# Stick-breaking values on the seven-product scheme, one weave over the mixer, and the mLSTM output kept in memory for a while

## The chip, the core and the metric

The kernel runs on one core of a Trainium2 chip, in one launch. The metric is the device time of the launch in microseconds; of the kernel before, three timed runs are shown and their median stands for it. The engines are named as in the profile: PE (matmuls, with PEld for its weight loads), DVE, ACT, POOL and SP; a "q" behind a name is the engine's queue, and almost all DMAs are issued from SP's. SBUF is the memory on the chip next to the engines, PSUM the buffers into which PE writes.

## The reference

One layer of a trunk over 256 positions of width 2048, all in float32: a SwiGLU block (2048 to 5632 and back), a layer norm, a mixer, a layer norm, a second SwiGLU block, a layer norm, and a gated embedding. The change lies in the mixer:

```
proj = x @ w_in                                   # (256, 2048) x (2048, 11272)
mq, mk, mv, mo, mi, mf, sq, sk, sv, ga, gb = split_cols(proj)
q_m, k_m = split(silu(causal_conv([mq, mk])))
h    = mlstm(q_m, k_m, mv, gates of mi, mf)       # 4 heads of 256
y_m  = head_norm(h) * sigmoid(mo)                 # (256, 1024)
y_sb = stick_breaking(sq, sk, sv)                 # 8 heads of 128, (256, 1024)
merged = sigmoid(ga) * (y_m @ w_up_m) + sigmoid(gb) * (y_sb @ w_up_sb)
mix = merged @ w_out
```

The stick-breaking attention needs, for each head, all of its q and k before its logits, and its v (sv) in its last product. The mLSTM needs its q, k, v and gates, and mo at its end.

## The kernel before, in words

**A unit of PE work.** Each float32 operand is split into a high and a low half, and a product takes three matmuls (high by high, high by low, low by high; lines 1209 to 1211). The smallest piece of the program is a `Unit`: one weight tile of 256 rows by up to 512 columns against 128 positions, which is 2 x 3 matmuls. A weight tile arrives by one DMA of 512 KB into a raw tile (`loads`, line 1132), ACT writes its high half (line 1160) and DVE its low half (line 1164). Both 128-position tiles use it, so in a plain `group` one load and one split serve two units.

**The seven-product scheme** (`seven`, `both7`) does two column groups of 512 over all 2048 rows with seven products of 2 x 2 blocks in place of eight: 7 x 4 = 28 units in place of 32. Each unit there has a weight tile of its own, and most of these tiles are sums that DVE makes in place (line 349). It also needs sums of the activations (`forms`), which `forms_later` makes from the tiles of x1T (lines 295 to 312). While such a block runs, five PSUM buffers hold its accumulators, and its results are put together from PSUM by ACT (line 400) and DVE (lines 384 and 390).

**The order.** `program` is one list of units and small callbacks. The code runs through it once and emits the instructions of every engine in that order. `sched` holds generators (the steps of an mLSTM head, a stick-breaking head, a transpose); each yields an estimated delay, and its next step is emitted when the units emitted so far add up to that time (line constants in `DELAY`). `until` runs steps early when a unit needs their result. `weave(main, side)` spreads the units of a side list evenly among those of a main list, by their numbers.

**The mixer before.** In a row, as plain groups: q and k of the mLSTM with the gates and the first stick-breaking heads, then v (two groups, line 795), mo (two groups), the first four heads of sv (line 683), and stick-breaking heads; the forms of x1T are made while these run; then the other half of sv. Only then comes the weave: main is the last stick-breaking columns, the gates of merge group 0, and the up products of groups 0 to 2 (`ups`), and side is the gates of groups 1 to 3 as three seven-product blocks (`pair`). The up products of group 3, the transposes of the merged groups (`merge_turn`) and w_out follow. The mLSTM heads run in two chains over the plain groups, and stick-breaking in two chains of four heads, at least 14 planned us apart, from before the weave until inside it.

**Buffers.** 48 SBUF pages of 4 KB per partition (`PAGES`) hold raw and split weights, activations and all the large tiles; a tile keeps its page until its last use. `HELD` limits the raw tiles and split pairs at a time: 5 and 6 in the mode "mix", 7 and 6 in "wide", which is that of the weave. Six `temp` tiles serve the small steps. PSUM has eight buffers (`PSUM_BUFS`), for accumulators and small steps (`misc`) alike. Early in the mixer the residual goes to DRAM and returns before w_out (`put_away`, line 252, and `bring_back`, line 260, on SP's queue).

**Lines of the small steps.** Stick-breaking: logits 888, running sums 901 and 902, their subtraction 903 on DVE, the output product 912, its halves 916 on ACT and 918 on DVE. mLSTM: the output product 844, its denominators 845 to 848 on DVE, the scaling out of PSUM on ACT (a call of line 228), transposes 870, halves 228 and 876. Transposes of q and k of stick-breaking: 693, with the copies 698.

Of the kernel before, what the change touches and what calls it, by code (L numbers as in the profile page):

```python
# [13 lines left out]
P = 128  # L14
# [29 lines left out]

STICK_GAP = 14.0
# [3 lines left out]
    "alpha": 24.0, "away": 5.0, "sig": 1.5, "form": 18.0, "ln_turn": 3.6, "ln_step": 2.1, "gb": 14.0, "h": 8.0, "silu": 6.0, "late": 9.0, "rest": 1.2, "mt": 3.2,  # L49
# [127 lines left out]
def kernel(  # L177
# [156 lines left out]
    def seven(wa, ca, wb, cb, rows, cols, act, done, loaded):  # L334
# [44 lines left out]
    def both7(w, ca, cb, act, dest, ready, loaded):  # L379
# [296 lines left out]
    def sb_columns(ps, t, heads):  # L676

        n = len(heads) * DS
        if heads[0] >= 16:
            if ("sv", t) not in st:  # L680
                st["sv", t] = big()
            c0 = (heads[0] - 16) * DS
            nc.scalar.copy(st["sv", t][:, c0:c0 + n], ps[:, :n])
            flags.update(("sv", t, h - 16) for h in heads)
        else:
            stage = temp()
            nc.scalar.copy(stage[:, :n], ps[:, :n])
            sched.spawn(sb_turn(t, stage, heads), DELAY["sbt"])
# [128 lines left out]

    def mlstm(h):
# [19 lines left out]
        r = small.tile([P, TT], F32, name="hr", tag="hr")  # L838
        hs = temp().rearrange("q (t e) -> q t e", t=TT)
        for t in range(TT):  # L840
            ps = misc([P, DM + 1])
            for s in range(t + 1):
                off = s * 256 + (t - s) * P
                nc.tensor.matmul(ps[:], d[:, off:off + P], st["v", s, h // 2][:, h % 2], start=(s == 0), stop=(s == t))  # L844
            nc.vector.tensor_scalar(out=r[:, t:t + 1], in0=ps[:, DM:], scalar1=-1.0, scalar2=st["em"][:, t, h:h + 1],
                                    op0=ALU.mult, op1=ALU.max)
            nc.vector.tensor_tensor(out=r[:, t:t + 1], in0=ps[:, DM:], in1=r[:, t:t + 1], op=ALU.max)
            nc.vector.reciprocal(out=r[:, t:t + 1], in_=r[:, t:t + 1])
            yield DELAY["m2"]
            activate(hs[:, t], ps[:, 0:DM], ACT.Copy, scale=r[:, t:t + 1])  # L850
# [79 lines left out]
    for which, g in ((0, 1), (1, 0), (1, 1)):  # L930
        program.extend(flat(group(w_in, range(0, D, 2 * P), which * 1024 + g * COL, COL, x1T, qk_done(which, g))))
    program.append(lambda: [sched.spawn(in_sequence([mlstm(a), mlstm(a + 1)])) for a in (0, 2)])
    for g in range(2):
        program.extend(flat(group(w_in, range(0, D, 2 * P), 2048 + g * COL, COL, x1T, v_done(g))))
    for g in range(2):
        program.extend(flat(group(w_in, range(0, D, 2 * P), 3072 + g * COL, COL, x1T, mo_done(g))))
    def sb(*heads):
        if heads[0] >= 16:
            col0 = sq0 + heads[0] * DS
        else:  # L940
            col0 = [(sq0 + h * DS, 2 * DS) for h in heads[::2]]
# [24 lines left out]
    def up_done(g, half):  # L966
        def done(ps, t):
# [3 lines left out]
            if half:  # L971
                m = gt[g, t][:, 0:COL]
                nc.vector.tensor_tensor(out=m, in0=m, in1=a, op=ALU.add)
# [4 lines left out]
    def merge_turn(g, t):  # L978
        transposed(gt[g, t], mergedT, g, t)
        return  # L980
        yield
# [4 lines left out]
    def ups(g):  # L986
        return (flat(group(w_up_m, range(0, HM * DM, 2 * P), g * COL, COL, ymT, up_done(g, 0)))
                + flat(group(w_up_sb, range(0, HS * DS, 2 * P), g * COL, COL, ysbT, up_done(g, 1))))
# [17 lines left out]
    def pair(g):  # L1006
        return both7(w_in, ga0 + g * COL, ga0 + D + g * COL, x1T, gate_dest(g), gate_ready(g), False)
# [239 lines left out]
```

## Time and profile before

| what | value |
| --- | --- |
| three runs | 2199.74, 2199.25, 2196.62 us; median 2199.25 us |
| the profiled execution's own time | 2198.95 us |
| its span, first to last instruction | 2196.9 us, so 2.05 us lie around it |
| mean granted PE clock | 0.999 |
| busy PE, DVE, ACT | 99%, 85%, 59% of the span |
| mLSTM q, k, gates (accumulators read) | 724 to 807 us |
| v, mo, sv, first stick-breaking columns | 808 to 1003 us |
| the weave | 1003 to 1283 us |
| last up products, w_out | 1283 to 1397 us |

The stages are read from the times at which ACT and DVE read the accumulators of each group. A line of the window view gives a stretch, its length, and for PE, PEld, DVE and ACT the busy time and, in brackets, the instructions, then the granted clock, the DMA engines' share and GB/s. A line of the group view gives the line, engine, operation, tiles, shapes and count, then busy us in total, mean ns of one, the idle time of the engine before them and who ended it.

### The profile page before, as it was taken

What the parts mean: (1) busy time and instruction counts of PE and PEld (TensorE: products, weight loads), DVE (VectorE), ACT (ScalarE), POOL (GpSimd) and SP (SyncE); (2) the same over time, 40 slices, a digit from 0 to 9 for tenths busy, and PEclk for the clock granted to TensorE, in tenths of its full rate; (3) what the DMA queues carried; (4) which work ended last, traced back from release to release, by engine and by line L of the source; (5) the groups of instructions that cost most, each with busy time, mean ns of one, the idle gap of its engine ahead of it and who ended that gap; (6) DMA issues with size and microseconds to landing.
All of it is one profiled execution on the core that took longest, in us unless ns stands there. A gap on an engine that the chain in (4) does not pass through costs nothing.

```text
span 2196.9 us, 28181 instructions
## 1 busy us (share of the span) xinstructions
PE 2183.5 (99%) x9990; PEld 1806.0 (82%) x9990; DVE 1867.9 (85%) x2073; ACT 1296.9 (59%) x1576; POOL 100.1 (5%) x88
## 2 busy tenths in 40 slices
PE   9999999999999999999999999999999999999999
PEld 7888888888888888888878888888888888878888
DVE  6999999999987864568978985699999899989774
ACT  7556566565655755565766554565665565656372
POOL 0100010000010000000000000000010000000000
PEclk9999999999999999999999999999999999999999
DMA  9899999999993765665768886589999999899553
GB/s 336 253 304 302 280 286 316 307 307 264 320 334 103 244 215 159 173 182 168 240 190 264 265 282 211 179 244 303 297 282 293 315 293 306 275 299 344 195 168 100
DMA packets 298893, 560.12 MB, mean 255 GB/s; under 512 B 18008, under 2 KB 39424, under 8 KB 298752
## 3 DMA queue, kind: packets, MB, share of 16 engines
q1 hardware_dynamic: 276992, 516.38, 70.8%
q0 software_dynamic: 21760, 41.95, 11.1%
q8 instruction: 78, 1.28, 0.2%
q14 instruction: 63, 0.52, 0.1%
HBM read 554.06 MB, written 4.19 MB: 254 GB/s over the span
## 4 chain that ended last, share of the span: by engine, by line
PE 66%; DVE 3%; DMA 3%; issue 1%; ACT 0%; POOL 0%; DVEq 0%; POOLq 0%; SPq 0%; ACTq 0%
PE mm L1209 21%; PE mm L1210 21%; PE mm L1211 21%; DMA raw<-in_ffn_w_dram 3%; DVE split L1164 2%; DVE raw L349 1%; PE ms L278 1%; PE ms L483 0%; ACT split L1160 0%; PE ms L888 0%; PE ms L832 0%; PE ms L844 0%; PE ms L912 0%; PE ms L901 0%; PE ms L693 0%
## 5 line engine op out<-in xcount | busy, mean ns | idle before, releaser
L1160 ACT CAST split<-raw 128x1024 fp32r<-128x1024 f32 (+2 forms) x1049 | 1046.2, 1037 | 512.6 <-DVE raw L349 171.0
L1164 DVE TENSOR_TENSOR split<-raw,split 128x1024 fp32r<-128x1024 f32 (+2 forms) x1049 | 1224.2, 1202 | 143.0 <-ACT split L1160 129.9
L1209 PE MATMUL mm<-split,actT 128*128 128x512 f32 (+2 forms) x3128 | 1219.9, 390 | 3.2 <-DVE temp L903 2.5
L1210 PE MATMUL mm<-split,actT 128*128 128x512 f32 (+2 forms) x3128 | 1206.2, 386 | 2.4 <-DVE split L1164 2.2
L1211 PE MATMUL mm<-split,actT 128*128 128x512 f32 (+2 forms) x3128 | 1206.5, 386 | 0.6 <-DVE actT L285 0.6
L1210 PEld LDWEIGHTS mm<-split,actT 128*128 128x128 f32 x3128 | 588.7, 188 | 120.4 <-DVE split L1164 7.5
L1211 PEld LDWEIGHTS mm<-split,actT 128*128 128x128 f32 x3128 | 588.0, 188 | 121.0 <-DVE actT L285 1.4
L1209 PEld LDWEIGHTS mm<-split,actT 128*128 128x128 f32 x3128 | 588.3, 188 | 119.2 <-issue 3.6
L349 DVE TENSOR_TENSOR raw<-raw 128x1024 f32<-128x1024 f32 x224 | 273.3, 1220 | 2.4 <-DMA raw<-in_w_in_dram 0.2
L1137 POOL DMA_DIRECT2D raw<-in_ffn_w_dram x80 | 95.5, 1193 | 1867.1 <-DVE temp L547 800.7
L280 ACT CAST actT<-ms 128x512 fp32r<-128x512 f32 x60 | 35.0, 585 | 87.0 <-PE ms L278 86.7
L556 DVE TENSOR_TENSOR temp<-mm,temp 128x512 f32<-128x512 f32 x112 | 76.9, 687 | 5.3 <-PE mm L1211 3.5
L609 DVE SCALAR_TENSOR_TENSOR big<-mm,big 128x512 f32<-128x512 f32 x96 | 65.5, 685 | 16.2 <-PE mm L1211 16.1
L285 DVE TENSOR_TENSOR actT<-ms,actT 128x512 fp32r<-128x512 f32 x60 | 40.8, 685 | 21.2 <-ACT actT L280 11.7
L224 ACT ACT_TABLE_LOAD x33 | 42.3, 1283 | 0.6
L273 DVE TENSOR_TENSOR actT<-temp,actT 128x512 fp32r<-128x512 f32 x40 | 26.5, 688 | 17.3 <-ACT actT L272 17.2
L228 ACT ACTIVATE temp<-mm 128x512 f32<-128x512 f32 (+1 forms) x22 | 12.3, 560 | 44.6 <-PE mm L1211 44.6
L272 ACT CAST actT<-temp 128x512 fp32r<-128x512 f32 x40 | 24.1, 621 | 13.8 <-DVE temp L296 11.9
L228 ACT ACTIVATE temp<-temp 128x512 f32<-128x512 f32 (+1 forms) x48 | 28.5, 593 | 2.2 <-DVE temp L556 1.7
L228 ACT ACTIVATE rstd<-mv,eps 128x1 f32<-128x1 f32 x6 | 1.8, 295 | 46.1 <-DVE mv L466 46.1
L782 DVE SCALAR_TENSOR_TENSOR temp<-ms,cw,temp 128x253 f32<-128x253 f32 (+2 forms) x48 | 22.4, 480 | 7.5 <-ACT temp L228 6.3
L1026 DVE SCALAR_TENSOR_TENSOR big<-big,mm 128x512 f32<-128x512 f32 x8 | 5.5, 687 | 26.9 <-PE mm L1211 26.9
(128 smaller groups left out, 557.4 us busy)
## 6 DMA issues: line engine op xcount, KB each, us to landing
raw<-in_ffn_w_dram SPq DMA_DIRECT2D x655, 512.0 KB, 6.3
raw<-in_w_in_dram SPq DMA_DIRECT2D x168, 512.0 KB, 4.4
raw<-in_ffn_w_dram POOLq DMA_DIRECT2D x80, 512.0 KB, 8.8
raw<-in_w_out_dram SPq DMA_DIRECT2D x32, 512.0 KB, 4.9
raw<-in_w_in_dram SPq DMA_DIRECT2D x56, 256.0 KB, 3.1
raw<-in_w_ple_gate_dram SPq DMA_DIRECT2D x24, 512.0 KB, 4.9
raw<-in_w_up_m_dram SPq DMA_DIRECT2D x16, 512.0 KB, 5.5
raw<-in_w_up_sb_dram SPq DMA_DIRECT2D x16, 512.0 KB, 5.6
```

Source lines behind the costliest of these rows:

```text
L224: nc.scalar.preload_act_table_set(table[0])
L228: nc.scalar.activation(out, in_, func, **kw)
L285: nc.vector.tensor_tensor(out=dst[:, 1], in0=ps[:], in1=dst[:, 0], op=ALU.subtract)
L349: nc.vector.tensor_tensor(out=out.tile[:, :, :cols], in0=a.tile[:, :, :cols], in1=b.tile[:, :, :cols], op=ALU.add)
L556: nc.vector.tensor_tensor(out=out, in0=a, in1=b, op=op)
L609: nc.vector.scalar_tensor_tensor(out=xs, in0=ps, scalar=0.5, in1=xs, op0=ALU.mult, op1=ALU.add)
L1137: nc.gpsimd.dma_start(out=r.tile[:, :, :r.cols], in_=r.plus[0], accum_op=ALU.add)
L1160: nc.scalar.copy(hi[:, ks], r[:, ks])
L1164: nc.vector.tensor_tensor(out=lo[:, ks], in0=r[:, ks], in1=hi[:, ks], op=ALU.subtract)
L1209: nc.tensor.matmul(ps, hi, w[0][:, k, :u.cols], start=first, stop=False)
L1210: nc.tensor.matmul(ps, hi, w[1][:, k, :u.cols], start=False, stop=False)
L1211: nc.tensor.matmul(ps, lo, w[0][:, k, :u.cols], start=False, stop=last)
```

## The change

- sv is no longer computed in two plain groups of 16 units each, whose results ACT copied. It becomes one seven-product block of 28 units (`both7(w_in, sv0, sv0 + COL, ...)`), with destination and readiness callbacks of its own.
- The weave starts earlier: behind the q and k groups. Main is v, mo, the stick-breaking columns, the gates of group 0 and the up products of groups 0 to 2; side is the block of sv and the three gate blocks. Mode "wide" holds from there.
- The forms of x1T are made one group earlier, 14 planned us apart instead of 18.
- The stick-breaking chains start behind the second group of mo.
- In the mLSTM the output product is copied out of PSUM by ACT with its denominators, and the reciprocal and the scaling follow from SBUF.
- When both halves of a tile of the mLSTM's output are ready, it goes to DRAM (four DMAs on SP's queue), and comes back ahead of the first up products, whose stick-breaking half now runs first in group 0.
- The merged groups share tiles: group 1 is written beside group 0 and group 3 beside group 2.
- The delay before a gate's sigmoid is 5.0 in place of 1.5.

```diff
-        if heads[0] >= 16:
...
-            nc.scalar.copy(st["sv", t][:, c0:c0 + n], ps[:, :n])
...
+    def put_ym_away(c, t):
+        nc.sync.dma_start(out=ym_rows(c, t), in_=ymT.tiles.pop((c, t))[:].bitcast(F32))
...
+    def bring_ym_back():
+        for c in range(2):
+            for t in range(TT):
+                ymT.tiles[c, t] = act_tile()
+                nc.sync.dma_start(out=ymT.tiles[c, t][:].bitcast(F32), in_=ym_rows(c, t))
...
-            nc.vector.tensor_scalar(out=r[:, t:t + 1], in0=ps[:, DM:], scalar1=-1.0, scalar2=st["em"][:, t, h:h + 1],
-                                    op0=ALU.mult, op1=ALU.max)
-            nc.vector.tensor_tensor(out=r[:, t:t + 1], in0=ps[:, DM:], in1=r[:, t:t + 1], op=ALU.max)
-            nc.vector.reciprocal(out=r[:, t:t + 1], in_=r[:, t:t + 1])
+            nc.scalar.copy(hs[:, t], ps[:, 0:DM])
+            nc.scalar.copy(den[:, t:t + 1], ps[:, DM:])
             yield DELAY["m2"]
-            activate(hs[:, t], ps[:, 0:DM], ACT.Copy, scale=r[:, t:t + 1])
+        nc.vector.tensor_scalar(out=r[:], in0=den[:], scalar1=-1.0, scalar2=None, op0=ALU.mult)
+        nc.vector.tensor_tensor(out=r[:], in0=den[:], in1=r[:], op=ALU.max)
+        nc.vector.tensor_tensor(out=r[:], in0=r[:], in1=st["em"][:, :, h], op=ALU.max)
+        nc.vector.reciprocal(out=r[:], in_=r[:])
+        yield DELAY["m2"]
+        for t in range(TT):
+            activate(hs[:, t], hs[:, t], ACT.Copy, scale=r[:, t:t + 1])
...
+            if ymT.ready(h // 2, t):
+                sched.spawn(put_ym_away(h // 2, t), DELAY["away"])
...
+    program.append(lambda: [sched.spawn(forms_later(x1T, c), FORMS + 14.0 * c) for c in range(4)])
...
-    program.extend(sb(16, 17, 18, 19))
-    program.append(lambda: [sched.spawn(forms_later(x1T, c), 6.0 + 18.0 * c) for c in range(4)])
-    program.extend(sb(8, 9, 2, 3))
...
+    def merged(g, t):
+        return gt[g // 2 * 2, t][:, g % 2 * COL:(g % 2 + 1) * COL]
...
-    program.append(sticks)
-    program.extend(sb(10, 11, 4, 5) + sb(20, 21, 22, 23))
-    main = sb(12, 13, 6, 7) + sb(14, 15) + branch(0, 0) + branch(0, 1) + ups(0) + ups(1) + ups(2)
+    main = columns(2048, v_done(0)) + columns(3072, mo_done(0)) + columns(2048 + COL, v_done(1)) + sb(8, 9, 2, 3)
+    main += columns(3072 + COL, mo_done(1)) + [sticks] + sb(10, 11, 4, 5) + sb(12, 13, 6, 7) + sb(14, 15)
+    main += branch(0, 0) + branch(0, 1) + [bring_ym_back] + ups(0, True) + ups(1) + ups(2)
+    sv0 = sq0 + 2 * HS * DS
+    side = both7(w_in, sv0, sv0 + COL, x1T, sv_dest, sv_ready)
     mode("wide")
-    program.extend(weave(main, pair(1) + pair(2) + pair(3)))
+    program.extend(weave(main, side + pair(1) + pair(2) + pair(3)))
```

More of the change, by code (lines that the diff above doesn't have):

```diff
@@ L332, in group, with seven @@
         return pairs
-    def seven(wa, ca, wb, cb, rows, cols, act, done, loaded):
+    def seven(wa, ca, wb, cb, rows, cols, act, done, loaded=False):
         n = rows // (4 * P)
@@ L678, in sb_columns @@
         n = len(heads) * DS
-        if heads[0] >= 16:
-            if ("sv", t) not in st:
-                st["sv", t] = big()
-            c0 = (heads[0] - 16) * DS
-            nc.scalar.copy(st["sv", t][:, c0:c0 + n], ps[:, :n])
[L684 to L688, printed above, removed]
+        stage = temp()
+        nc.scalar.copy(stage[:, :n], ps[:, :n])
+        sched.spawn(sb_turn(t, stage, heads), DELAY["sbt"])
     def sb_turn(t, stage, heads):
@@ L838, in mlstm @@
         r = small.tile([P, TT], F32, name="hr", tag="hr")
+        den = small.tile([P, TT], F32, name="den", tag="den", bufs=2)
         hs = temp().rearrange("q (t e) -> q t e", t=TT)
@@ L929, with columns, sv_dest, sv_ready @@
     program.extend(flat(group(w_in, range(0, D, 2 * P), 4096, 2 * HM + 2 * DS, x1T, gates_done)))
[L930 to L931 removed]
+    def columns(col0, done):
+        return flat(group(w_in, range(0, D, 2 * P), col0, COL, x1T, done))
+    program.extend(columns(COL, qk_done(0, 1)) + columns(1024, qk_done(1, 0)))
+    program.append(lambda: [sched.spawn(forms_later(x1T, c), FORMS + 14.0 * c) for c in range(4)])
+    program.extend(columns(1024 + COL, qk_done(1, 1)))
     program.append(lambda: [sched.spawn(in_sequence([mlstm(a), mlstm(a + 1)])) for a in (0, 2)])
[L933 to L936, printed above, removed]
     def sb(*heads):
[L938 to L941, printed above, removed]
+        col0 = [(sq0 + h * DS, 2 * DS) for h in heads[::2]]
         return flat(group(w_in, range(0, D, 2 * P), col0, len(heads) * DS, x1T,
                           lambda ps, t: sb_columns(ps, t, heads)))
[L945 to L947 removed]
+    def sv_dest(k, t):
+        if ("sv", t) not in st:
+            st["sv", t] = big()
+        return st["sv", t][:, k * COL:(k + 1) * COL]
+    def sv_ready(k, t):
+        flags.update(("sv", t, h) for h in range(4 * k, 4 * k + 4))
     def sticks():
@@ L970, in done @@
             nc.vector.tensor_tensor(out=a, in0=ps, in1=a, op=ALU.mult)
-            if half:
-                m = gt[g, t][:, 0:COL]
-                nc.vector.tensor_tensor(out=m, in0=m, in1=a, op=ALU.add)
+            if last:
+                nc.vector.tensor_tensor(out=merged(g, t), in0=gt[g, t][:, 0:COL], in1=gt[g, t][:, COL:], op=ALU.add)
                 if g == 3:
@@ L978, in merge_turn @@
     def merge_turn(g, t):
-        transposed(gt[g, t], mergedT, g, t)
+        transposed(merged(g, t), mergedT, g, t)
         return
```

25 lines of the change are left out of this document (18 added, 7 removed).

## The prediction

> **What bounds the kernel now.** I read the page first, then the view of busy time by stretches, then the chain of waits and the time line around the places where PE stood.
>
> ```profile
> PE 2183.5 (99%) x9990; PEld 1806.0 (82%) x9990; DVE 1867.9 (85%) x2073; ACT 1296.9 (59%) x1576; POOL 100.1 (5%) x88
> ```
> ```profile
> 100.00:600.00 500.00, 499.61 (x2234) 411.96 (x2232) 473.70 (x466) 300.04 (x319) 41.68 (x35) 1.00 0.97 297
> 808.00:1003.00 195.00, 195.00 (x885) 160.15 (x884) 119.24 (x197) 108.58 (x155) 0.00 (x0) 1.00 0.59 167
> 1003.00:1283.00 280.00, 276.76 (x1279) 229.90 (x1277) 251.19 (x271) 180.05 (x226) 0.00 (x0) 0.99 0.76 232
> 808.00:1283.00 475.00, 471.76 (x2163) 390.05 (x2161) 370.43 (x468) 288.63 (x381) 0.00 (x0) 1.00 0.69 206
> ```
>
> PE is the bound: it stands for only 13.4 us (2196.9 - 2183.5), so time falls only with PE's own work or with those 13.4 us. In the plain groups (808 to 1003 us) PE never stands and DVE is busy 61% (119.24 / 195). In the weave (1003 to 1283) DVE is busy 90% and PE loses 3.24 us. The price of one matmul of 512 columns is read from starts in the time line:
>
> ```profile
> 1087.17 0.39 PE L1209 MATMUL mm<-split,actT 128*128 128x512 f32 x1
> ...
> 1090.12 0.39 PE L1210 MATMUL mm<-split,actT 128*128 128x512 f32 x1
> ```
>
> Thirteen steps lie between them: 2.95 / 13 = 0.227 us each (the 0.39 overlaps the next one and is no price), so a unit of six costs 1.36 us. The places where PE stood, by stretches, the last row inside the third:
>
> ```profile
> 1050.00:1060.00 10.00, 9.26 (x56) 7.99 (x56) 7.56 (x9) 7.64 (x15) 0.00 (x0) 1.00 0.64 186
> 1060.00:1080.00 20.00, 20.00 (x120) 17.61 (x119) 19.67 (x22) 13.07 (x20) 0.00 (x0) 1.00 0.83 251
> 1130.00:1140.00 10.00, 7.58 (x35) 6.04 (x33) 9.89 (x10) 4.62 (x5) 0.00 (x0) 1.00 0.80 253
> 1140.00:1150.00 10.00, 9.93 (x37) 8.03 (x38) 6.64 (x8) 4.36 (x7) 0.00 (x0) 0.83 0.37 102
> 1142.00:1144.00 2.00, 2.00 (x6) 1.60 (x5) 2.00 (x4) 1.04 (x1) 0.00 (x0) 0.50 0.54 88
> ```
>
> From 1130 to 1140 DVE is busy 9.89 of 10 us and PE loses 2.42. The chain of waits says why:
>
> ```profile
> 1135.85 1.23 DVE split L1164
> ...
> 1138.24 1.22 DVE split L1164
> 1139.46 0.47 DVE temp L903
> 1139.94 0.14 issue
> 1140.07 0.47 PE mm L1209
> ```
>
> A stick-breaking subtraction (903), which frees a PSUM buffer, stands in DVE's queue behind weight splits, and PE's next accumulator needs a buffer. Of the eight, the seven-product block holds five and the main group two, so one is left for all small steps. The time lost: 0.74 (1050 to 1060) + 2.42 + 0.07, and in the third row 17% of 10 us at the lower clock, 1.7: together **4.9 us**. The clock's row shows 0.50 behind a gap of 2.5 us. (The Trainium skill, "TensorE: Matmul & The Clock Gate", section "What's actually happening", has PE fall to half its clock after an idle window of about 3.4 us. By that rule this gap would have cost no clock and the 4.9 would be 3.2; the measured 0.50 decides.)
>
> **The change, part by part.**
>
> ```profile
> L1164 DVE TENSOR_TENSOR split<-raw,split 128x1024 fp32r<-128x1024 f32 x195 | 233.7, 1220 | 66.3 <-ACT split L1160 62.3 <-PE mm L1210 3.2
> L349 DVE TENSOR_TENSOR raw<-raw 128x1024 f32<-128x1024 f32 x48 | 58.5, 1219 | 0.5 <-DMA raw<-in_w_in_dram 0.2
> L384 DVE TENSOR_TENSOR big<-mm,big 128x512 f32<-128x512 f32 x18 | 12.4, 686 | 0.2
> L1160 ACT CAST split<-raw 128x1024 fp32r<-128x1024 f32 x197 | 200.7, 1050 | 72.8 <-DVE raw L349 26.4 <-PE mm L1210 16.0 <-DVE split L1164 14.2
> ```
>
> *sv by seven products.* 32 units become 28: 4 x 6 x 0.227 = **5.4 us less of PE**, the only certain term, since PE is the bound. Against it: 28 weight tiles are split in place of 16, 12 x 1.22 = 14.6 us of DVE and 12 x 1.05 = 12.6 of ACT; 16 sums of weights, 16 x 1.22 = 19.5 of DVE; and results put together in 7 DVE instructions of 0.686, 4.8. So DVE gets 39 us, ACT 13 (less three copies). Loads rise from 16 to 24.
>
> *One weave.* Main grows from 112 to 208 units, side from 84 to 112. What hides the 39 us of DVE is PE's time over the longer weave: with the mLSTM's small saving (below), (370.4 + 37.5) / (475 - 10) = 88%, against the weave's 90% before and 95% in the first SwiGLU (473.7 / 500), where PE stood for 0.39 us in 500. More to the point is the worst place. A side unit costs DVE 1.22 + 16/28 x 1.22 + 7/28 x 0.686 = 2.09 us. In the half-wide group (heads 14, 15) 16 main units of half price come with 12 side units before: DVE 8 x 0.69 + 12 x 2.09 = 30.6 us to PE's 16 x 0.68 + 12 x 1.36 = 27.2, or 112%, which is the full DVE from 1060 on. After, 8.6 side units come with them: 23.5 to 22.6, 104%. In an up group (16 main units, six DVE results) it was 39.0 to 38.1, 102%, and becomes 31.9 to 33.5, 95%. So DVE's queue should be short where stick-breaking's small steps wait in it, and I take the 4.9 us as gone. What is late next is again a PSUM buffer in the half-wide group.
>
> *mLSTM in the weave.* PE's work is the same. Three small DVE operations for each tile become four for each head:
>
> ```profile
> L845 DVE TENSOR_SCALAR hr<-ms,em 128x1 f32<-128x1 f32 x8 | 1.7, 219 | 16.6 <-PE ms L844 16.6
> L848 DVE RECIPROCAL hr<-hr 128x1 f32<-128x1 f32 x8 | 1.3, 165 | 0.3
> L687 ACT COPY temp<-mm 128x256 f32<-128x256 f32 x2 | 0.7, 362 | 0.0
> ```
>
> 24 operations of about 0.18 become 16: 1.4 us less. ACT gets eight copies of 256 columns (0.36) and eight of one (not shown; at most that 0.36): 3 to 6 us, at 288.6 + 16 of 465 busy, 66%, hidden behind PE. These copies free the PSUM buffer without DVE. The head takes two planned steps longer; nothing waits for it before the up products. But its PSUM steps now stand where seven buffers are taken: the risk of this part.
>
> *Output in memory.* Eight DMAs of 512 KB on SP's queue, with eight more loads of sv: 16 x 0.52 = 8.4 MB to 206 GB/s x 475 us = 98 MB, so 229 GB/s where the first SwiGLU runs at 297. Raw loads queue behind them. The residual is the nearest, waits of SP from 700 to 820 and 1150 to 1310 us:
>
> ```profile
> SPq L252 <- DVE big L511: 13.9, 3, 5.7
> SPq L260 <- PE mm L1211: 0.4, 1, 0.4
> raw<-in_w_in_dram SPq DMA_DIRECT2D x168, 512.0 KB, 4.4
> ```
>
> 5.7 us at the longest, where seven raws at 2.2 us each (200 loads in some 440 us) last 15: nothing on the path. Without that cover PE would lose the wait itself, up to 5.7 each.
>
> *Order.* The forms' 17 us of DVE move ahead of 840 us, where the plain groups left DVE 39% idle; they are planned at 10 to 52 us behind q and k, and needed from about 50 on. Stick-breaking has 72 + 43 = 115 units x 1.297 planned us = 149 until the up products read it, and its chains need 108 + 31 = 140. Both cost nothing; if the chains were late, `until` would emit steps early and PE would stand for them. Packing the merged groups and the sigmoid's delay change places and times, not work.
>
> *New waits.* The trace does not show mLSTM inside a weave, so it is bounded from both sides. Below: the first SwiGLU's 0.4 us. Above: the old rate for each buffer taken.
>
> ```profile
> L888 PEld LDWEIGHTS ms<-big 128*128 128x128 f32 x24 | 4.1, 190 | 1.3 <-ACT big L698 1.0
> L901 PE MATMUL ms<-temp,tri 128*128 128x384 f32 x12 | 4.8, 485 | 0.0
> ```
>
> The old weave had six logits, six sums, eight outputs and four transposes, 24 takes, for 4.9 us. The new one has 24 of stick-breaking, 8 transposes and 4 x 6 of mLSTM, 56: 11.4 us. By DVE's share (88%) the nearest row is the old weave, but its worst places fall by 7 or 8 points; I take half of what it lost, **2.5 us**.
>
> **Sum** against the profiled execution: 2198.95 - 5.4 - 4.9 + 2.5 = 2191.1; the median of the runs stands 0.3 above that execution, so 2191.4, said as **2191 us**. If the waits merely stay as they are, 2198.95 - 5.4 = 2193.5, still faster.
>
> **The rivals.** *Waits at the old rate.* The 56 takes each cost what the 24 did: 2198.95 - 5.4 - 4.9 + 11.4 = 2200. For it: mLSTM's scores (line 834) and its output halves (876) free their buffers only through DVE, so 28 takes wait for DVE in place of 14. Against it: the 95% busy DVE of the first SwiGLU, also with five buffers held and with small steps, cost 0.39 us.
>
> *Raw weights come late: slower.* Where v, mo and the first heads are worked on, the pages asked for are 16 for x1T and its forms, 7 raw, 12 split, 10 of q, k, v and mo, 2 of gates and 2 of sq and sk, 49, and with sv and the first output 53, less those of heads that are done; there are 48. A load that finds no page waits on SP until PE is done with an old split, and fewer loads are under way. From issue to use a raw takes 4.4 + 1.05 + 1.22 + 1.22 = 7.9 us, so at one load in 2.2 us 3.6 must be under way; from three on it decides: 7.9 / 3 = 2.63, 0.43 more for each of the 46 loads between main units 32 and 80, 20 us: 2211. For it:
>
> ```profile
> SPq L1132 <- PE mm L1211: 92.7, 39, 7.5
> DVE raw L349 <- DMA raw<-in_w_in_dram: 0.2, 1, 0.2
> ```
>
> SP does wait for PE's pages (1150 to 1310 us). Against it: by the same count the old weave asks for 52 at 1125 us (16 + 19 + 4 mLSTM outputs + 2 sv + 2 sq, sk + 4 stick-breaking outputs + 5 gates), and in the mixer's weave the engines waited for a load only these 0.2 us; four pages go to memory for the late part.
>
> **How the numbers follow.** The forecast, from 2187 to 2194.8, has 0.68: 5.4 us are sure, and 4.4 us (0.2%, about what a measurement of this kernel can tell from no change) are reached unless waits grow by a us. Waits at the old rate have 0.16, all within 0.2%; late raws 0.16, slower. The low end is the sum with the lowest waits, 2189, less 2 for the spread of runs (2196.62 to 2199.74 before). The high end reaches over the old rate to 2204; most of the late raws and a few hundredths below are left out, under 0.2.
>
> **What would show it.** Right: 24 fewer matmuls of 512 columns, 12 more splits and 16 more sums at line 349; in the half-wide and up groups DVE under full; no granted clock under 1 in the weave; one short wait of PE for a small step's PSUM buffer at most. Old rate: several waits of PE for 903, 918, 834 or 876 with the clock at 0.50 behind them. Late raws: DVE's and ACT's waits for the DMA of raw between 840 and 1000 us, with PE idle in each row there. The prediction is wrong altogether if DVE shows over 95% through the first half of the weave, or PE waits for v or mLSTM steps emitted early.

## The result, and the profile after

The changed kernel takes **2217.15 us** (median of four runs, 2214.71 to 2218.26) beside 2198.51 us for the kernel before (four runs, 2196.62 to 2199.74): ratio 1.0084 [1.0071, 1.0097], 18.6 us slower where 8 us faster was forecast. The profiled execution took 2217.22 us, with a span of 2215.5 us.

The engine totals of the changed kernel, from the first part of its page:

```profile
PE 2185.7 (99%) x9966; PEld 1805.1 (81%) x9966; DVE 1902.6 (86%) x2100; ACT 1313.7 (59%) x1603; POOL 100.1 (5%) x88
```

PE has 24 instructions fewer (9966 for 9990), so the seven-product saving is there; but the span less PE's busy time is now 2215.5 - 2185.7 = 29.8 us, where it was 13.4. Two groups carry DVE's part, the first from the page, the second from the view that keeps shapes apart:

```profile
L1195 DVE TENSOR_TENSOR split<-raw,split 128x1024 fp32r<-128x1024 f32 (+2 forms) x1061 | 1239.9, 1203 | 152.2 <-ACT split L1191 130.2
```
```profile
L352 DVE TENSOR_TENSOR raw<-raw 128x1024 f32<-128x1024 f32 x240 | 293.0, 1221 | 2.8 <-DMA raw<-in_w_in_dram 0.7 <-DMA raw<-in_ffn_w_dram 0.2
```

There are 12 splits more (1061 for 1049) and 16 sums more (240 for 224), as counted, and DVE grew by 1902.6 - 1867.9 = 35 us (39 had been worked out). Now the stretches of the changed kernel's weave, with the columns as told ahead of the prediction:

```profile
840.00:940.00 100.00, 92.54 (x392) 74.52 (x392) 77.94 (x105) 57.70 (x77) 0.00 (x0) 0.95 0.59 179
940.00:1040.00 100.00, 95.68 (x421) 78.26 (x421) 76.76 (x91) 62.49 (x88) 0.00 (x0) 0.97 0.71 220
1040.00:1140.00 100.00, 94.88 (x478) 78.93 (x477) 80.68 (x106) 70.31 (x107) 0.00 (x0) 1.00 0.68 208
1140.00:1240.00 100.00, 96.80 (x432) 79.77 (x432) 77.38 (x87) 61.84 (x76) 0.00 (x0) 1.00 0.75 235
...
1000.00:1020.00 20.00, 15.68 (x60) 11.95 (x59) 12.65 (x18) 11.49 (x19) 0.00 (x0) 0.83 0.43 139
...
1200.00:1283.00 83.00, 83.00 (x369) 68.80 (x368) 76.38 (x75) 47.61 (x51) 0.00 (x0) 1.00 0.84 272
```

The kernel before, in the rows that are not full there:

```profile
1040.00:1140.00 100.00, 96.84 (x485) 81.04 (x483) 86.47 (x99) 69.56 (x98) 0.00 (x0) 1.00 0.74 222
1140.00:1240.00 100.00, 99.93 (x435) 82.59 (x436) 89.30 (x89) 60.01 (x66) 0.00 (x0) 0.98 0.78 243
```

The loss is spread over 840 to 1200 us and is gone from there on, when the mLSTM and stick-breaking heads are done. From 840 to 1240 PE stands for 20.1 us and loses another (0.05 + 0.03) x 100 = 8 us to the lower clock. Before, the same stretch lost 3.2 us and, with rows of 1.00 and 0.98, 2. The difference, 16.9 + 6, less 5.4 of matmuls, is 17.5 of the 18.6 us. **In a stretch where PE loses 4.3 us, DVE is not full**: 12.65 of 20 us from 1000 to 1020. But such a share hides what happens in the waits themselves. Over PE's waits alone DVE is busy for 14.4 of the 20.1 us: nearly all the time before 861.11, about half of it before 1011.54.

```profile
856.92:861.11 4.19, 0.01 (x1) 0.01 (x1) 4.09 (x6) 2.42 (x3) 0.00 (x0) 1.00 0.54 159
1008.58:1011.54 2.96, 0.00 (x0) 0.00 (x1) 1.64 (x3) 2.22 (x5) 0.00 (x0) 0.96 0.61 177
```

The waits of PE from 690 to 1420 us (us in total, times, longest):

```profile
PE ms L890 <- DVE actT L896: 4.9, 2, 3.0
PE ms L910 <- DVE actT L940: 4.3, 3, 2.0
PE ms L859 <- DVE temp L848: 4.2, 1, 4.2
PE ms L836 <- DVE actT L896: 2.7, 2, 1.4
...
```

All are small steps (`ms`), none a main accumulator. L859 (mLSTM's output product) waits for its operand, the scores that DVE multiplies in 848. In all the others the releaser belongs to another step: in the longest, transposes (890), logits (910) or an mLSTM head's first product (836) wait until DVE's 896 or 940 has read the step before out of PSUM. They wait for the one free buffer. The time line shows one of each kind:

```profile
853.95 1.23 DVE L1195 TENSOR_TENSOR split<-raw,split 128x1024 fp32r<-128x1024 f32 x1 [3.71 <-ACT split L1191]
...
860.49 0.56 DVE L848 SCALAR_TENSOR_TENSOR temp<-ms,temp 128x384 f32<-128x384 f32 x1
...
861.11 1.23 PE L859 MATMUL ms<-big,temp 128*128 128x257 f32 x2 [4.19 <-DVE temp L848]
...
1007.87 1.28 ACT L227 ACT_TABLE_LOAD   x1
...
1008.20 0.38 PE L890 MATMUL ms<-ident,temp 128*128 128x128 f32 x2
1009.16 0.52 ACT L231 ACTIVATE temp<-temp 128x384 f32<-128x384 f32 x1
1009.72 0.61 ACT L231 ACTIVATE temp<-temp,ones 128x384 f32<-128x384 f32 x1
1010.24 0.60 ACT L231 ACTIVATE actT<-ms,cw 128x128 fp32r<-128x128 f32 x2
1010.88 0.61 DVE L896 SCALAR_TENSOR_TENSOR actT<-ms,cw,actT 128x128 fp32r<-128x128 f32 x2 [1.27 <-ACT actT L231]
1011.54 0.69 PE L890 MATMUL ms<-ident,temp 128*128 128x128 f32 x2 [2.96 <-DVE actT L896]
1012.26 0.62 ACT L231 ACTIVATE actT<-ms,cw 128x128 fp32r<-128x128 f32 x2 [1.42 <-PE ms L890]
1012.92 0.61 DVE L896 SCALAR_TENSOR_TENSOR actT<-ms,cw,actT 128x128 fp32r<-128x128 f32 x2 [1.44 <-ACT actT L231]
1013.59 1.22 PE L836 MATMUL ms<-big 4*128 4x256 f32 x2 [1.36 <-DVE actT L896]
```

From 1008 to 1014 three steps take turns in one buffer. The first transposes are done at 1008.6, but ACT is loading a table (1.28 us) and then does two operations of a stick-breaking head; its copies come at 1010.24, DVE's at 1010.88, the next transposes at 1011.54. DVE waited there (1.27 and 1.44 us). PE, ACT and DVE run one after the other. From start to start such a **round trip** takes 2.05 us (1011.54 to 1013.59), and 3.34 with the table and the other head's operations in it, and all matmuls queued behind the step on PE wait with it. At 861 DVE is late with the scores: PE had made them by 851.4, but DVE stood 3.71 us for a split from ACT, and from 853.95 on it worked off three splits, a sum and some of the forms before it came to 848 at 860.49.

### The profile page after: what moved, and what is told of

Read it like the earlier page. It is cut to its first block, busy times and chain, and to the rows that moved or that the text cites. A ratio compares the mean times of both kernels' runs of the same rounds, so it can differ in the third digit from the quotient of the medians.

```text
span 2215.5 us, 28239 instructions
## 1 busy us (share of the span) xinstructions
PE 2185.7 (99%) x9966; PEld 1805.1 (81%) x9966; DVE 1902.6 (86%) x2100; ACT 1313.7 (59%) x1603; POOL 100.1 (5%) x88
## 3 DMA queue, kind: packets, MB, share of 16 engines
q8 instruction: 78, 1.28, 0.2%
## 5 line engine op out<-in xcount | busy, mean ns | idle before, releaser
L1191 ACT CAST split<-raw 128x1024 fp32r<-128x1024 f32 (+2 forms) x1061 | 1059.0, 1037 | 535.1 <-DVE raw L352 168.1
L1195 DVE TENSOR_TENSOR split<-raw,split 128x1024 fp32r<-128x1024 f32 (+2 forms) x1061 | 1239.9, 1203 | 152.2 <-ACT split L1191 130.2
L352 DVE TENSOR_TENSOR raw<-raw 128x1024 f32<-128x1024 f32 x240 | 293.0, 1221 | 2.8 <-DMA raw<-in_w_in_dram 0.7
L227 ACT ACT_TABLE_LOAD x35 | 44.9, 1283 | 0.6
L1057 DVE SCALAR_TENSOR_TENSOR big<-big,mm 128x512 f32<-128x512 f32 x8 | 5.5, 688 | 26.9 <-PE mm L1242 26.9
L231 ACT ACTIVATE temp<-ms,gbT 128x128 f32<-128x128 f32 x64 | 24.1, 459 | 5.5 <-PE ms L486 5.5
```

Of the source, the lines that this page charges most:

```text
L227: nc.scalar.preload_act_table_set(table[0])
L231: nc.scalar.activation(out, in_, func, **kw)
L352: nc.vector.tensor_tensor(out=out.tile[:, :, :cols], in0=a.tile[:, :, :cols], in1=b.tile[:, :, :cols], op=ALU.add)
L1191: nc.scalar.copy(hi[:, ks], r[:, ks])
L1195: nc.vector.tensor_tensor(out=lo[:, ks], in0=r[:, ks], in1=hi[:, ks], op=ALU.subtract)
```

## The experiments

The theory after this reading: the loss is waits for the one free PSUM buffer, made by small steps that follow each other too closely, and steps put on PE's queue before their operands are there. The rival: DVE's load (and ACT's) is the cause, as the prediction had it. The runs, each beside runs of the kernel before on the same chip (whose median lay between 2198.4 and 2199.7), with PE's idle time and clock from 840 to 1240 us (400 less the busy time of that stretch):

| run | median us | ratio to before | idle us, clock |
| --- | --- | --- | --- |
| before | 2198.5 | 1 | 3.2, 1.00 |
| after | 2217.2 | 1.0084 [1.0071, 1.0097] | 20.1, 0.98 |
| e1_share | 2200.7 | 1.0002 [0.9992, 1.0011] | 8.9, 0.98 |
| e2_nosums | 2205.5 | 1.0028 [1.0018, 1.0038] | 13.7, 0.99 |
| e3_spaced | 2202.9 | 1.0018 [1.0009, 1.0028] | 11.2, 0.99 |
| e4_mlstm_before | 2225.4 | 1.0118 [1.0103, 1.0133] | 28.0, 0.97 |
| e5_spaced_ready | 2197.3 | 0.9992 [0.9982, 1.0001] | 8.3, 1.00 |
| e6_plain_sv | 2218.5 | 1.0085 [1.0070, 1.0100] | 14.4, 0.97 |
| **e7_before_spaced** | **2196.1** | **0.9986 [0.9976, 0.9995]** | 0.6, 1.00 |
| e8_scores_only | 2217.9 | 1.0086 [1.0071, 1.0101] | 21.5, 0.97 |
| e9_best | 2212.8 | 1.0060 [1.0048, 1.0073] | 15.6, 0.98 |
| e10_best_wider | 2201.2 | 1.0010 [1.0001, 1.0019] | 9.8, 0.99 |
| e11_half_gap | 2204.7 | 1.0025 [1.0016, 1.0034] | 11.7, 0.98 |
| e12_best_nosums | 2201.8 | 1.0012 [1.0003, 1.0021] | 9.9, 0.99 |
| e13_two_takes | 2209.6 | 1.0043 [1.0028, 1.0058] | 15.8, 0.99 |
| e14_two_takes_18 | 2202.0 | 1.0010 [1.0000, 1.0020] | 11.3, 1.00 |
| e15_two_takes_13 | 2203.4 | 1.0016 [1.0007, 1.0025] | 11.1, 0.99 |
| e16_ready_18 | 2206.9 | 1.0035 [1.0022, 1.0048] | 15.8, 0.99 |
| e17_ready_13 | 2208.9 | 1.0042 [1.0028, 1.0056] | 15.1, 0.99 |
| e18_ready_share | 2200.5 | 1.0005 [0.9995, 1.0014] | 10.5, 0.99 |

### A second free buffer, or a lighter DVE

e1 lets two of the five held accumulators share a PSUM buffer, so the weave leaves two free; the number of operations is the same, and the seven-product results of the mixer are other numbers.

```diff
         accs = {m: {} for m in range(1, 8)}
+        if not loaded:
+            accs[7] = accs[5]
...
```

> The changed kernel, with products 5 and 7 of the mixer's seven-product blocks accumulated in one PSUM buffer instead of two (so sv and the gates come out as other numbers; matmuls, splits, sums and evictions stay as many). A block then holds four buffers and the small steps have two. Theory (small steps that follow each other on PE take turns in one free buffer, and PE waits a round trip through ACT and DVE for each): most of the waits from 840 to 1180 us go, some 29 us of idle and slow clock fall under 10, time 2198 us, 2194 to 2203. Rival (the waits are DVE's queue, long with splits and sums): nothing changes, 2213 to 2218.

e2 leaves out the DVE sums of raw weights in the mixer's seven-product blocks (64 x 1.22 = 78 us of DVE; the 88 sums of the second SwiGLU stay), so that those products use other weights.

```diff
         def plus(out, a, b):
+            if not loaded:
+                return None
```

> The changed kernel without the in-place sums of weight tiles in the mixer's seven-product blocks (its results are other numbers): 64 DVE additions of 1.22 us, 78 us, are left out, and everything else stays. Theory (one free buffer): the round trips stay, each a bit shorter; 2206 to 2215 us. Rival (DVE's queue): with a fifth of DVE's work gone from the weave the waits go, 2195 to 2202 us.

With the second buffer nearly all came back: 1.0084 - 1.0002 of the time, 18 us. Its remaining waits of PE:

```profile
PE ms L841 <- DVE actT L901: 4.4, 2, 2.7
PE ms L864 <- DVE temp L853: 4.2, 1, 4.2
PE ms L694 <- DVE actT L945: 0.2, 1, 0.2
```

The data wait of 4.2 stayed to the digit. Without the sums 11.7 us came back, 0.5 us under what the theory had left room for (2206) and 3.5 above the rival's 2195 to 2202. The data wait went; the buffer waits stayed nearly as long as they were:

```profile
PE ms L893 <- DVE actT L899: 4.3, 2, 3.0
PE ms L913 <- DVE actT L943: 4.2, 3, 2.0
PE ms L839 <- DVE actT L899: 2.7, 2, 1.4
...
```
```profile
1000.00:1020.00 20.00, 15.97 (x61) 12.45 (x62) 9.27 (x14) 8.43 (x14) 0.00 (x0) 0.83 0.42 121
```

From 1000 to 1020 DVE is now busy 9.27 of 20 us, and PE stands for 4.0 us all the same (4.3 after). Over e2's waits alone DVE is busy for 6.8 of 13.7 us, so the waits for the buffer do not need a full DVE. Of the 6.4 us of idle time that went (20.1 to 13.7), 4.2 are the data wait. So the buffer is the larger cause, and DVE's load a second one, above all where it delays the scores of the first mLSTM heads. The two gains, 18 and 11.7 us, add up to more than the 18.6 lost, so they are not separate shares of it.

### Spacing the steps

e3 is the changed kernel with one addition: a step that takes a PSUM buffer comes at least 2.6 planned us behind the last one (from the first up products on with one raw tile and one split pair fewer held). e7 puts the same addition into the kernel before.

```diff
+    def take():
+        due = max(sched.now, st.get("take", 0.0))
+        st["take"] = due + TAKE_GAP
+        yield due - sched.now
...
+        yield from take()
         ps = misc([P, 2, P])
```

> The changed kernel, same results, with each small step of mLSTM and stick-breaking that takes a PSUM buffer planned at least 2.6 us behind the last one, so that PE has units of the products to do between two takes (and one raw tile and one split pair less from the first up products on, for the pages). Theory (neighbours that take turns in one buffer): waits fall to under 10 us, 2195 to 2204 us. Rival (DVE's queue holds the buffer wherever the step stands): 2211 to 2218 us. Third (steps emitted before their data are there, as at 856 us): only the buffer waits move, the one of 4 us stays.

> The kernel before, with the spacing of small steps of e3 (2.6 planned us) and nothing else. Theory (its waits at 1053 and 1137 us are buffer waits): 4 to 5 us less than the kernel before, 2194 us. Rival (DVE full from 1060 and 1130 on): no difference, 2199 us, or a new long wait where the chains become late.

e3 won back 14.2 us by the medians. Counted in the time line, 22 of the changed kernel's 56 small steps in the weave start less than 2.5 us behind the one before, and three more would have but for their own waits (2.96, 2.01 and 1.14 us); in the weave before it is 9 of 25, with the spacing 1 of 56. What is left in e3 is mostly waits for data:

```profile
PE ms L950 <- DVE temp L821: 4.5, 1, 4.5
PE ms L871 <- DVE temp L859: 4.2, 1, 4.2
...
```

L950 is a stick-breaking output emitted before its mask (821) was done, because the first up products read it: the spaced chains end too late. In e7 both waits of before are gone, and the row of 1040 to 1140 us, which had 96.84 busy, is full:

```profile
1040.00:1140.00 100.00, 100.00 (x500) 83.91 (x499) 89.60 (x102) 72.59 (x102) 0.00 (x0) 1.00 0.73 224
```

It is the fastest kernel here, faster than both: 0.9986, about 3 us, where the prediction had put those waits at 4.9. DVE's share rose (89.60 for 86.47) while PE stopped waiting.

e11 halves the spacing of e3:

```diff
-TAKE_GAP = 2.6
+TAKE_GAP = 1.3
```

> The kernel after with the spacing alone, 1.3 planned us in place of the 2.6 of the spaced run (2202.9). Theory (a wait is what is left of a round trip of 2 to 3 us when the next step comes): about half of the 14.2 us comes back, 2208 to 2212. Rival (any small displacement breaks the pattern): 2203, as with 2.6. Other rival (the spacing worked by moving steps to other places): no gain, 2215 to 2218.

It lost 1.8 us of the 14.2 by the medians, with intervals that overlap, and not half: near the first rival's number. Nine of 56 steps start within 2.5 us there, yet the waits for 909 and 956 sum to under 3 us. The wait is thus not simply what is left of a round trip.

### One part at a time

e4 puts v and mo back into plain groups ahead of the weave (with the forms behind them, and 6 raw tiles and 5 split pairs held), so that mLSTM runs mostly outside.

```diff
+    program.extend(columns(2048, v_done(0)) + columns(3072, mo_done(0)) + columns(2048 + COL, v_done(1)))
+    program.extend(columns(3072 + COL, mo_done(1)))
...
+    main = sb(8, 9, 2, 3) + sb(10, 11, 4, 5) + [sticks] + sb(12, 13, 6, 7) + sb(14, 15)
```

> The changed kernel with v and mo as plain groups before the weave, so that mLSTM runs where only the main group's accumulators are held; sv stays on seven products; side units per main unit rise from 0.54 to 0.88 (and one raw tile and one split pair less in the weave, for the pages). Theory (one free buffer): mLSTM's waits, some 18 us with the clock, go and stick-breaking's stay or grow a little: 2197 to 2206 us. Rival (DVE's queue): the weave is denser, DVE at 96%, and time does not fall: 2215 us or more.

The theory's number was missed by far: 8 us slower than after, which is the rival's number (2215 or more).

```profile
PE ms L910 <- DVE actT L940: 10.1, 2, 6.5
PE ms L890 <- DVE actT L896: 5.8, 1, 5.8
...
PE ms L934 <- DVE temp L812: 3.5, 1, 3.5
...
```

These are waits in the same buffer, but of 5.8 and 6.5 us (ending at 971.5 and 1075.2). DVE is busy for 5.41 of the 5.50 us from 966 to 971.5 and for 8.93 of the 9 from 1066 to 1075: the step's eviction stands in its queue behind splits, sums and forms. Over all waits from 840 to 1240 DVE is busy for 26.9 of 28.0 us, although its share of the stretch is 78%. So here the rival's cause is right as well: the length of a wait is the round trip plus the queues, and the weave made denser paid more for each. e6 has sv in two plain groups, on top of e5 (below), to price the seven products by themselves:

```diff
+    main += columns(sv0, sv_done(0)) + columns(sv0 + COL, sv_done(1)) + sb(8, 9, 2, 3)
...
-    side = both7(w_in, sv0, sv0 + COL, x1T, sv_dest, sv_ready)
+    side = []
```

> The kernel of e5 with sv as two plain groups of 16 units in the main list instead of the seven-product block (results the same up to rounding). 24 matmuls more. If PE's work is the price once the waits are gone: 5.4 us over e5, 2194 us. Rival (the block's 39 us of DVE and its five buffers cost more than its matmuls save): at or under e5.

At 2218.5 us it missed both numbers and doesn't give that price, since stick-breaking's chains came late, and PE waited and lost its clock at the first up products:

```profile
1140.00:1240.00 100.00, 92.53 (x390) 74.77 (x389) 65.00 (x76) 62.54 (x82) 0.00 (x0) 0.91 0.62 194
```

e8 is the changed kernel with the planned time of mLSTM's score product at 7.0 in place of 4.0, so that the 4.2 us wait at 861 goes:

```diff
-    "m0": 4.0, "m1": 4.0, "m2": 2.0, "m3": 4.6, "m4": 4.6, "sa": 1.4, "s0": 7.0, "s1": 9.0, "s2": 3.0, "s3": 5.0, "s4": 6.0,
+    "m0": 4.0, "m1": 7.0, "m2": 2.0, "m3": 4.6, "m4": 4.6, "sa": 1.4, "s0": 7.0, "s1": 9.0, "s2": 3.0, "s3": 5.0, "s4": 6.0,
```

> The changed kernel with one number changed: mLSTM's output product is planned 7.0 us behind its scores in place of 4.0. If the wait at 856 us is a wait for data of its own: about 6 us less with the clock, 2211 us, 2208 to 2213. If PE only loses the time at the next step instead: 2215 to 2219 us.

No gain, the second number. The wait of 4.2 became two of 1.5, and the transposes' waits grew from 4.9 to 6.5 us: removed alone, it came back elsewhere.

### Spacing with data ready, and other orders

e5 is e3 with the score product at 7.0 and stick-breaking's chains started ahead of the second mo group, 16 main units earlier:

```diff
-    main += columns(3072 + COL, mo_done(1)) + [sticks] + sb(10, 11, 4, 5) + sb(12, 13, 6, 7) + sb(14, 15)
+    main += [sticks] + columns(3072 + COL, mo_done(1)) + sb(10, 11, 4, 5) + sb(12, 13, 6, 7) + sb(14, 15)
```

> The spaced kernel, same results, with mLSTM's output product planned 7.0 us behind its scores in place of 4.0, and the stick-breaking chains started 16 main units earlier, behind the third stick-breaking columns. The spaced kernel kept two long waits of PE for data of steps emitted too early (855 us, scores from DVE; 1187 us, the last two heads pushed out together by the up products), 7 us each with the slow clock. Theory (free buffers and data, not DVE's load): both go, 2189 us, 2186 to 2195. Rival (DVE's queue sets it): the waits come back at other steps, 2198 us or more.

2197.3 us is 20 us better than after and the best form of the change, but no faster than before beyond the interval, and some 8 us above what the theory gave. What is left of PE's waits:

```profile
PE ms L950 <- DVE temp L821: 4.4, 2, 2.5
PE ms L846 <- DVE actT L909: 1.9, 2, 1.1
PE ms L871 <- DVE temp L859: 1.5, 1, 1.5
...
```

Next came the second mo group behind heads 10, 11, 4, 5, and both output transposes of an mLSTM head in one buffer (e9 and e10, spaced 2.2 and 2.6; e12 is e9 without the DVE sums, left out as in e2):

```diff
+        yield from take()
+        both = misc([P, TT, 2, P])
...
+    main += [sticks] + sb(10, 11, 4, 5) + columns(3072 + COL, mo_done(1)) + sb(12, 13, 6, 7) + sb(14, 15)
```

> The kernel after with the takes of the one free PSUM buffer spaced (2.2 planned us), mLSTM's score product given 7.0 planned us in place of 4.0, both of a head's output transposes in one buffer (8 takes fewer), stick-breaking's chains begun 32 main units earlier (the second mo group behind heads 10, 11, 4, 5), 30 held tiles in the last part as in the spaced runs. Theory (the 18.6 us are waits in one free buffer, and steps put on PE's queue too early): by PE's work alone 24 matmuls less, 5.4 us, so 2192 if a few us of waits remain as in the spaced run with ready data (2197, whose last heads were forced out for 4.6 us): 2188 to 2195, faster than before. Rival (the even weave's DVE load keeps some us of waits whatever the spacing): 2196 to 2200, no change from before.

> The same with the spacing at 2.6 planned us in place of 2.2: the last heads are forced out 3.4 planned us early where the first up products read them, in place of 0.8. Theory: within 2 us of the run with 2.2, slower if anything (the forced steps stand on PE): 2190 to 2197. Rival (what counts is the room between takes): faster than it by a us or more.

> The spaced and reordered kernel with the 64 DVE sums of raw weights left out in the mixer's weave and the second SwiGLU (78 us of DVE's work; the output holds other numbers). Theory (with the takes apart and the data ready, DVE's load costs the mixer next to nothing): within 3 us of the same kernel with the sums, what is left of its short waits. Rival (DVE's load is the cause and the spacing only hides a part of it): 6 us or more faster than it, and than 2186.

e9 was 18 us above the theory's range and e10, with 0.4 us more room, 11.7 better than e9, as its rival had it. e12 (its expectation names the second SwiGLU too, but the 64 sums left out are all the mixer's) was 11 us faster than e9, the rival's first number, though it didn't reach 2186. Between 840 and 940 us the sums cost e9 7 us of idle time and clock, which e12 does not lose; but from 1020 to 1060 us e12 stands as e9 does:

```profile
1020.00:1060.00 40.00, 30.71 (x120) 23.67 (x119) 23.66 (x34) 22.96 (x32) 0.00 (x0) 0.87 0.50 147
```

DVE busy 59%, ACT 57%, PE idle for 9.3 us: here it is waits and not load over the stretch. e13 to e15 are e9 with a buffer for each transpose again, spaced 2.2, 1.8 and 1.3 (`TAKE_GAP`), the last with the score product at 9.0:

> The 2212.8 us kernel (spacing 2.2, second mo group behind heads 10, 11, 4, 5) with a head's two output transposes in a PSUM buffer each again, everything else the same. Theory (the merged transposes hold the one free buffer through four copies on ACT and four products on DVE, in place of two and two, and the 3.9 and 1.8 us waits behind them are that hold): those waits go, 2194 to 2202. Rival (the order of main, with its dense stretch at 1020 to 1070 us, is what lost the time): 2208 to 2214.

> The same with the spacing at 1.8 planned us: no step is forced out before the first up products. Theory: 2192 to 2200, at most 2 us from the run with 2.2. Rival (order of main): 2208 to 2214, as there. Other rival (room between takes counts): 3 us or more slower than with 2.2.

> The same with the spacing at 1.3 planned us and mLSTM's score product given 9.0 planned us in place of 7.0. Theory: the data wait of 1.5 us for mLSTM's output goes; 2192 to 2200. Rival (order of main): 2208 to 2214.

e13 (2209.6) has the rival's number, so the shared buffer had cost little of that time (3.2 us). But the order of the groups did not either, or not alone: e14, with the same order and less room, is 7.6 us faster than e13, although 6 of its steps start within 2.5 us and none of e13's. e14 and e15 missed every range given for them, by 2 to 6 us. e16 and e17 take e5's order again, spaced 1.8 and 1.3, e17 with the score product at 9.0 (their expectations speak of one buffer for both transposes; in the kernels that ran each has its own, so e16 differs from e5 in the spacing alone), and e18 adds e1's second buffer to e16; its seven-product results are other numbers, as in e1.

> The kernel of the 2197.3 us run (takes spaced, mLSTM's score product given 7.0 planned us, stick-breaking's chains begun earlier, main's order as in the change otherwise) with both output transposes of an mLSTM head in one PSUM buffer and the spacing at 1.8 planned us in place of 2.6, so that three of stick-breaking's last steps are forced out early in place of eight. Theory (what was left in that run is 6.7 us at the forced last heads and 4 us in the first mLSTM heads): 2191 to 2195. Rival (any order of the takes loses some 8 to 10 us more than before in the weave): 2196 to 2202.

> The same with the spacing at 1.3 and mLSTM's score product given 9.0 planned us. Theory: the wait for that product goes as well, 2190 to 2195. Rival: 2196 to 2202, as with 1.8.

> The kernel with the spacing at 1.8 and, as in the first run of this study, products 5 and 7 of the mixer's seven-product blocks in one PSUM buffer, which leaves two buffers for the small steps in place of one (the results of these blocks hold other numbers; PE, DVE and ACT do the same work). Theory (the change's loss is the one free buffer and steps emitted before their data are there, nothing else): both are gone, so the change keeps its 24 matmuls, 5.4 us, and before's 4.9 us of waits: 2186 to 2191. Rival (DVE's and ACT's load in the denser weave costs PE some us of its own): 2194 to 2198.

e16 and e17 missed both numbers (9.5 and 11.6 us above e5). e18 gained 6.4 us over e16 but stays 9.5 above the theory's range and 2.5 above the rival's. From 940 to 1040 us its PE is busy 100.00 of 100; what is left is:

```profile
PE ms L955 <- DVE temp L826: 5.3, 1, 5.3
PE ms L929 <- DVE actT L961: 2.1, 1, 2.1
PE ms L876 <- DVE temp L864: 1.5, 1, 1.5
```
```profile
1185.33 1.05 ACT L1212 CAST split<-raw 128x1024 fp32r<-128x1024 f32 x1 [1.91 <-DMA actT<-ymaway]
1186.40 1.28 ACT L230 ACT_TABLE_LOAD   x1
...
1187.69 0.52 ACT L234 ACTIVATE temp<-temp 128x384 f32<-128x384 f32 x1
...
1189.18 2.54 DVE L1216 TENSOR_TENSOR split<-raw,split 128x1024 fp32r<-128x1024 f32 x2 [1.54 <-ACT split L1212]
1191.64 0.42 DVE L826 TENSOR_TENSOR temp<-temp,bound 128x256 f32<-128x256 f32 x1
```

The last heads are late: their exponential (234) stands in ACT's queue behind a table load and a split that, by the view, waits 1.9 us for mLSTM's output coming back from memory. It is done at 1188.2, but the mask (826) comes only at 1191.64, behind two splits in DVE's queue. So the theory in its strict form ("the buffer and too early steps in the middle, nothing else") falls; the end of stick-breaking's chains is the third place. Which placement of the takes is good in detail is **not settled**: of the four comparisons that differ in the spacing alone, the narrower one was 9.5 us worse (e16 for e5), 11.7 worse (e9 for e10), 1.8 worse (e11 for e3, no clear difference) and 7.6 better (e14 for e13).

## Why the prediction was wrong, point by point

1. *PE is the bound, 0.227 us a matmul, and 24 are saved.* Right as a count (9966 for 9990). No run prices the 5.4 us alone (e6 could not).
2. *The old waits, 4.9 us, caused by a PSUM buffer that a small step holds.* Right in its place: e7 removed them with nothing but spacing and gained 3 us.
3. *DVE 39 us, ACT 13 more, hidden.* The sizes were near (35 measured for DVE, 17 for ACT with the mLSTM's copies). Hidden only in part: without 78 us of DVE's sums 11.7 us came back, of which the 4.2 us wait for mLSTM's scores was a plain case of DVE being late.
4. *The even weave has DVE under full in the half-wide and up groups, so the 4.9 us are gone.* This step failed. DVE's share did fall (80.68 and 77.38% in the rows of 1040 to 1240, from 86.47 and 89.30), and PE's idle time there rose from 3.2 to 8.3 us. DVE's share does not price a wait in a single buffer: with DVE at 46% (e2) it was as long as with 63%. In the waits themselves DVE was busy for 14.4 of 20.1 us, so its queue at that moment counts, not its mean.
5. *mLSTM in the weave: copies on ACT free the buffer without DVE; the risk of this part.* The risk was the main thing: 11.8 of the 20.1 us of idle time, and all 8 of clock, lie from 840 to 1040 us, while the forecast had the next wait in the half-wide group. The copies did free the output product's buffer without DVE, but heads of mLSTM and stick-breaking now stood side by side in the one buffer that is left, and one product was emitted 4.2 us before its scores were there, which the prediction had named as a sign against itself.
6. *Output in memory, nothing on the path.* Right in the changed kernel, whose row of 1200 to 1283 us is full. In e18, where the return falls on the last heads, it is, by the view, 1.9 us of a wait.
7. *Chains, 140 of 149 planned us, cost nothing.* Right for the change as it stands; the margin was too thin for any repair by spacing (4.5 us in e3, 4.4 in e5, 5.3 in e18).
8. *New waits 2.5 us, between 0.4 and 11.4.* **The term that decided, mis-sized by some 26 us**: 20.1 us of idle time and 8 of clock from 840 to 1240 in place of 2.5. The upper bound was not one: it took before's 0.2 us for each step, but both the neighbours and their price grew. Steps that come within 2.5 us of the one before, but for their own wait, went from 9 to 25, and such a pair cost 4.9 / 9 = 0.5 us before and (20.1 - 4.2 + 8) / 25 = 1.0 after, if all but the one data wait is put down to them. Why the pair's price grew is open in part; table loads and full queues ahead of an eviction, as at 1008 and in e4, are two reasons seen.

The rival of waits at the old rate named the right releasers (its lines 834, 876 and 918 are 848, 896 and 940 in the changed kernel) at the old price, with a clock of 0.50 behind some of them, as seen. The rival of late raws didn't come: from 840 to 1283 us DVE's sums waited 0.7 us for them (the row of 352) and its splits 1.5, and no wait of PE was put down to a load. A safer bound, an estimate from counts that only the trace gave, would have been a round trip for each step that comes so close: 25 x 2.05 = 51 us. Even that holds only where the queues are short, as e4's single wait of 6.5 us shows.

## What to carry to other kernels

When the accumulators leave one PSUM buffer for everything else, count the small steps that follow each other within one round trip of eviction (here 2 to 3 us) and price those, whatever the evicting engines' busy shares over a longer stretch say; what counts is what stands in their queues when the step comes. Spread the steps before adding work to such a weave, and see that the chain they form still ends before its reader: the gain of 3 us in e7 came from that alone. A repair in one place is judged by the whole stretch, since a removed wait came back elsewhere (e8).

## What the runs showed of the hardware

Whether a gap costs clock depends on more than its length. Granted clock of the changed kernel behind a gap of 4.19 us (ending at 861.11), behind 2.96 and 1.36 with 0.69 of work between (ending at 1013.59), behind one of 2.01 (ending at 1168.76), and in the last row that of e13 behind one of 2.79 (ending at 1045.38):

```profile
862.00:864.00 2.00, 2.00 (x6) 1.53 (x6) 2.00 (x3) 1.38 (x3) 0.00 (x0) 0.50 0.00 0
...
1015.00:1017.00 2.00, 2.00 (x5) 1.55 (x6) 0.47 (x1) 1.50 (x3) 0.00 (x0) 0.50 0.00 0
...
1170.00:1172.00 2.00, 2.00 (x10) 1.65 (x9) 0.47 (x1) 1.98 (x4) 0.00 (x0) 1.00 0.02 9
...
1046.00:1048.00 2.00, 2.00 (x10) 1.64 (x9) 1.91 (x3) 1.31 (x2) 0.00 (x0) 1.00 0.76 248
```

Half the clock until about 864.5 behind the first and until about 1018 behind the second, none lost behind the third and the fourth. Yet the kernel before had 0.50 behind a single gap of 2.49 us, and e9 0.50 (1047 to 1049) behind one of 1.79 ending at 1045.44. What else decides is open. (The Trainium skill, "TensorE: Matmul & The Clock Gate", section "A second HAM failure mode: psum-queue depth-cycling", tells of a kernel whose clock falls through many short gaps between groups of matmuls. The second row fits that, since its pieces were under 3 us each; the third shows that one gap of 2 us was harmless.) In the changed kernel the lower clock added 8 us to 20.1 of waiting.

The 35 table loads of ACT took 1.28 us each (33 before); with one of them and two other operations ahead of the copies, the round trip at 1008 took 3.34 us, where the next took 2.05.
